# Hybrid decoder layer on one core: forms of the down projection and squared norms of the mixer, re-ordered

## The chip, the cores and the metric

One core of a Trainium2 chip runs the whole inference step as one program. The metric is device time in microseconds. The kernel is written with a scheduling layer: the program's functions emit instructions with priorities, the layer puts them into five in-order queues, one for each of TensorE (PE, matrix products), VectorE (DVE), ScalarE (ACT), GpSimd (POOL) and SyncE (SP, which issues nearly all DMAs), and adds the waits between them. An instruction that waits holds up all that stand behind it in its queue.

## The reference, cut to what matters

```
def l2_normalize(x):
    return x * lax.rsqrt(jnp.sum(x * x, axis=-1, keepdims=True) + 1e-6)
...
    q = l2_normalize(qkv[:, :, 0])                       # 4 heads x 128, after a short conv and silu
    k = l2_normalize(qkv[:, :, 1])
    o, s_new = gated_delta_chunked(q, k, v, g, beta, s0) # per head: triangular solve, then a scan over chunks
...
    x = x + jnp.square(jax.nn.relu(rms_norm(x, g_ff) @ w_up)) @ w_down
    x = x + (p @ w_ple) * jax.nn.sigmoid(rms_norm(x, g_ple) @ w_ple_gate)
```

There are 1024 prompt tokens and 8 sample tokens, the model width is 1024, the MLP is 4096 wide, all float32. The change touches three things in it: the norms of q and k in each of the four heads, the product with w_down, and the input embedding p.

## The kernel before, in words

Every float32 product is made as three reduced-precision products: a weight tile is split into a rounded part `whi` (a cast on ACT, L150) and a rest `wlo` (a subtraction on DVE, L153), the activations likewise, and PE adds hi·hi, lo·hi and hi·lo. A weight tile in this split pair is called a form (`form`, L169). The forms come out of a ring of four (`RING`), so ACT and DVE work a few tiles ahead of PE.

The mixing stage runs head by head inside the input projection. `weave` is a planner: it counts the PE time of the projection's matmuls and lets other generators ("tasks") emit their next piece when their due time, given by the costs that they yield (`NRM`, `RB_W`, `MRG` and others), has come. Hence the costs set the place of an instruction on every queue. For each head `gdn_gates` transposes k (and q) on PE, forms the sum of squares of every token in `ssf` (L564 adds the epsilon), takes a reciprocal root by 11 tiny DVE instructions (`rsqrt`, L248 to L254, called "the root" here), and multiplies by beta into `rkb`. PE transposes `rkb` (`rbT`, L578); from there a matrix `at` is built, `gdn_inverse` inverts its 32x32 blocks by 62 POOL instructions (L643, L644), writes the result to DRAM (`inv_d`), reads it back as `t`, transposes four blocks of it on DVE (L657, `STREAM_TRANSPOSE`) and merges the blocks by small matmuls (`m`, L667 and L676). `gdn_scan` then goes through eight chunks, with PE, DVE (`R` L716, `vn` L724, `st` L730) and ACT (`vk` L722) taking turns.

The down projection uses a fast scheme of seven half-size products for each quarter j of the 4096 rows: 28 products n = 0 to 27, in the order P1, P6, P7, P4, P2, P5, P3. Each product has four column blocks p, and each block is 24 matmuls. Its activations come from DRAM (`load_raw`, 1.06 MB in two halves), are cast on ACT (L1363) and their rest formed on DVE (L1364). Its weights are the raw quarter blocks A11, A21, A22, A12 (`load_a`, 1 MB each) or sums of them made on POOL: `s1` = A21+A22 (L1385) and `s2` = s1-A11 (L1386) for P6, `sd` (L1392) for P7 and P3. PE's and SP's order is the program's; ACT, DVE and POOL are ordered by the scheduler with `high_priority`, and by `tc.issue_after(x)`, which puts an instruction on its queue behind x.

While the products run, other work is woven in. The last two tiles of the up projection are still to be squared (`squared`, L1225, on ACT) and turned into differences (`dforms_of`, six POOL instructions, L1229 to L1231). The old residual comes in by `x1_old` (L1401, two DMAs of about 520 KB each, called for the four quarters C11, C21, C12, C22 of the result). After n = 12 the embedding p is loaded (`pt`, L1526), and each of its eight 128x256 pieces is scaled on POOL (L1530).

Of the kernel before, what the change touches and what calls it, by code (L numbers as in the profile page):

```python
# [9 lines left out]
F32 = mybir.dt.float32  # L10
# [7 lines left out]
P = 128  # L18
# [66 lines left out]
def trunk_step_kernel(  # L85
# [199 lines left out]
    with ExitStack() as mix:  # L285
# [255 lines left out]
        def gdn_gates(h, kq):  # L541

            q, k = kq[:, 1, :T], kq[:, 0, :T]
            hb = slice(h * NU, h * NU + NU)
            ck_put(h, 0, k)
            dt = sr.tile([P, T], F32, tag="dt", name="dt")
            SY.dma_start(dt, gc_d[h, :].partition_broadcast(P))
            ktok = sr.tile([P, T], F32, tag="kt", name="ktok")
            ssf = sm.tile([P, 2 * NU], F32, tag="ss", name="ssf")
            for j, src in ((0, k), (1, q)):  # L550
                for u0 in (0, 4):
                    ps = transposes(src, u0, "kT")
                    if j == 0:
                        V.tensor_copy(ktok[:, u0 * P : u0 * P + 512], ps)
                    for a in range(4):
                        u = u0 + a
                        sq = tn.tile([P, P], F32, tag="oq", bufs=1, name="sq")
                        x2 = ps[:, a * P : a * P + P] if j else ktok[:, u * P : u * P + P]
                        with tc.high_priority(PRI):
                            S.activation(sq, x2, AF.Square, accum_out=ssf[:, j * NU + u : j * NU + u + 1])  # L560
                    yield NRM
            ck_put(h, 2, ktok[:, :])
            with tc.high_priority(PRI):
                V.tensor_scalar_add(ssf, ssf, 1e-6)  # L564
                rkq = sm.tile([P, 2 * NU], F32, tag="rkq", bufs=4, name="rkq")
                rsqrt(sm, rkq, ssf, "rk")
                rk, rq = rkq[:, :NU], rkq[:, NU:]
                V.tensor_scalar_mul(rq, rq, P ** -0.5)
                rkb = sm.tile([P, NU], F32, tag="rkb", name="rkb")
                V.tensor_mul(rkb, rk, beta[:, h, :NU])  # L570
            nrke = sm.tile([P, NU], F32, tag="nrke", bufs=4, name="nrke")
            V.scalar_tensor_tensor(nrke, in0=rkb, scalar=-1.0, in1=eg[:, hb], op0=ALU.mult, op1=ALU.mult)
            rkl = sm.tile([P, NU], F32, tag="rkl", bufs=4, name="rkl")
            V.tensor_mul(rkl, rk, el[:, hb])
            gs[h] = dict(rq=rq, nrke=nrke, rkl=rkl)
            yield RB_W
            ps = pst("rbT", (NU, P))
            PE.transpose(ps, rkb, ident)  # L578
            rbr = sm.tile([NU, P], F32, tag="rbr", name="rbr")
            V.tensor_copy(rbr, ps)  # L580
            SY.dma_start(rb_d[h : h + 1, :].rearrange("o (u c) -> (o u) c", c=P), rbr)
            at = sr.tile([P, T], F32, tag="at", bufs=2, name="at")
            SY.dma_start(at, rb_d[h, :].partition_broadcast(P))
# [12 lines left out]
            for u in range(0, NU, 2):
                ps = pst("kk")
                for a in range(2):
                    c = slice((u + a) * P, (u + a + 1) * P)
                    PE.matmul(ps[:, a * 256 : a * 256 + 256], lhsT=k[:, c], rhs=kq[:, :, c], start=True, stop=True)  # L600
                for a in range(2):
                    c = slice((u + a) * P, (u + a + 1) * P)
                    r = rk[:, u + a : u + a + 1]
                    V.scalar_tensor_tensor(at[:, c], in0=ps[:, a * 256 : a * 256 + P], scalar=r, in1=at[:, c],
                                           op0=ALU.mult, op1=ALU.mult)
                    V.scalar_tensor_tensor(dt[:, c], in0=ps[:, a * 256 + P : a * 256 + 256], scalar=r, in1=dt[:, c],
                                           op0=ALU.mult, op1=ALU.mult)
# [16 lines left out]
        def gdn_inverse(h, at):  # L624
# [28 lines left out]
            td = [t64[Q[0], :, 0:32], t64[Q[1], :, 32:64], t64[Q[2], :, 0:32], t64[Q[3], :, 0:32]]  # L653
            for b in range(4):
                SY.dma_start(td[b], inv_d[1, h, b].rearrange("u i j -> i u j"))
            for b in range(4):
                V.transpose(sf3[Q[b], :, Q[b]], td[b])  # L657
            xp = sm.tile([P, NU, 64], F32, tag="xp", bufs=1, name="xp")

            def j32(ap):  # L660
# [716 lines left out]
    def down_forms():  # L1377
        for j in range(4):
            s1 = dst.tile([P, 4, 4, P], F32, tag="s1", name="s1")
            s2 = dst.tile([P, 4, 4, P], F32, tag="s2", name="s2")  # L1380
            for name, _ in DSTEPS:
                for p in range(4):
                    with tc.high_priority(PRI):
                        if name == "P6":
                            G.tensor_add(s1[:, p], a_of("A21", p), a_of("A22", p))  # L1385
                            placed["sum"] = G.tensor_sub(s2[:, p], s1[:, p], a_of("A11", p)).ins  # L1386
                            f = s2[:, p]
                        elif name == "P5":
                            f = s1[:, p]
                        elif name in ("P7", "P3"):  # L1390
                            f = dst.tile([P, 4, P], F32, tag="t", name="sd")
                            G.tensor_sub(f, *((a_of("A21", p), a_of("A11", p)) if name == "P7" else (a_of("A12", p), s2[:, p])))  # L1392
                        else:
                            f = a_of({"P1": "A11", "P4": "A22", "P2": "A12"}[name], p)
                        f = form(f)
# [53 lines left out]
        return q // 2 * 4 + 2 * nn + q % 2  # L1449

    def down():
        load_raw(0)
        load_a(0, "A11")
        load_a(0, "A21")
        load_a(0, "A22")
        x1_old(C11, 0, 0)
        split_raw(0)
        load_raw(1)
        source = down_forms()
# [1 line left out]
        for n, (j, i) in enumerate(seq):  # L1461
# [4 lines left out]
            for p in range(4):  # L1466
# [16 lines left out]
                f = next(source, None)  # L1483
                if f:
                    forms.append(f)
                if n == 1 and p < 2:
                    _, t, q = last[p]
                    with tc.issue_after(placed["cast", 1]):
                        squared(q)
                    with tc.issue_after(placed["sum"]):  # L1490
                        dforms_of(t, q, late[t])
                if j == 3:

# [23 lines left out]
                x1_old(C21, 1, 0)  # L1517
            elif n == 1:
                x1_old(C12, 0, 1)
            elif n == 2:  # L1520
                for p, t, q in last:
                    dforms_out(p, t, q, late[t])
            elif n == 3:
                x1_old(C22, 1, 1)
            elif n == 12:
                SY.dma_start(pt, p_prompt[0, 0].rearrange("(c p) d -> p c d", p=P))  # L1526
            elif 14 <= n < 18:
                for nn in range(2):
                    x = pt[:, pcol(nn, n - 14), :]
                    G.tensor_scalar_mul(x, x, mst[:, nn, n - 14 : n - 13])  # L1530
            if j < 3:
                for name in {1: ("A11", "A21"), 2: ("A22",), 5: ("A12",)}.get(i, ()):
                    load_a(j + 1, name)
# [275 lines left out]
```

## Time and profile before

| what | value |
|---|---|
| runs | 1405.53, 1400.80, 1403.98 us, median 1403.98 |
| profiled execution: time, span | 1404.94 us, 1403.2 us |
| busy | PE 94%, DVE 64%, POOL 51%, ACT 46% |
| mean granted TensorE clock | 0.971 |
| DMA | 194 MB, 138 GB/s on average |

PE is nearly always busy. What is left are some stalls of PE and stretches in which PE runs at the lower of its clock's two levels, 1.2 instead of 2.4 GHz (granted clock 0.50). In a row of a timeline the columns are the start, the duration, the engine, the line and the operation with its output and inputs; what stands in square brackets is how long the engine was idle just before, and what ended that.

### The profile page before, as it was taken

The numbers are of one execution on the slowest core, as the hardware profiler recorded it, in microseconds if no ns is written. First come the engines' busy times: TensorE is split into PE (matmuls) and PEld (weight loads), VectorE is DVE, ScalarE is ACT, GpSimd is POOL, SyncE is SP. The second block draws the span as 40 slices with busy tenths as digits, with TensorE's granted clock in tenths as the row PEclk, the third lists the DMA queues.
The fourth block names the chain that finished last, engine by engine and source line by source line (L and its number), as shares of the span: only waits on it lengthen the run. The fifth ranks groups of instructions, "written<-read, shape, count | busy, mean of one in ns | idle before, by whom it ended". The sixth has DMA issues, their size and how long they took to land.

```text
span 1403.2 us, 26599 instructions
## 1 busy us (share of the span) xinstructions
PE 1312.5 (94%) x10189; PEld 1280.5 (91%) x10189; DVE 900.7 (64%) x1836; ACT 645.6 (46%) x1353; POOL 708.8 (51%) x724
## 2 busy tenths in 40 slices
PE   6979978999999799899999999889998999899996
PEld 5879978888999799899999999889998999899996
DVE  7755745456946856555545544567976878797554
ACT  7574645632232415556545445443332333346344
POOL 5300888847515404668856787350516215835241
PEclk9999988999999999999999999999999999999998
DMA  7334534646524831244455564658353533232231
GB/s 237 101 91 107 153 92 137 177 135 174 150 84 146 259 90 46 61 137 130 150 149 169 175 212 155 221 191 283 117 184 113 172 122 121 61 102 78 63 121 61
DMA packets 213419, 194.00 MB, mean 138 GB/s; under 512 B 20952, under 2 KB 183451, under 8 KB 213284
## 3 DMA queue, kind: packets, MB, share of 16 engines
q1 hardware_dynamic: 213292, 192.30, 44.5%
q8 instruction: 80, 1.31, 0.4%
q14 instruction: 47, 0.39, 0.1%
HBM read 131.75 MB, written 60.61 MB: 137 GB/s over the span
## 4 chain that ended last, share of the span: by engine, by line
PE 69%; DVE 9%; POOL 9%; ACT 5%; issue 4%; DMA 3%; SPq 1%; POOLq 0%; ACTq 0%; DVEq 0%
PE A L1184 10%; PE D L1184 7%; PE d L1474 6%; PE d L1475 6%; PE d L1473 6%; PE g L209 5%; PE g L211 5%; PE g L210 5%; PE B L1184 3%; PE C L1184 3%; POOL xinv L644 2%; PE g L1702 2%; POOL it L643 2%; DVE wlo L153 2%; PE g L1704 2%
## 5 line engine op out<-in xcount | busy, mean ns | idle before, releaser
L209 PE MATMUL g<-ra,whi 128*128 128x384 f32 (+3 forms) x800 | 272.6, 341 | 0.7 <-ACT ra L388 0.6
L1474 PE MATMUL d<-h,wlo 128*128 128x260 f32 (+1 forms) x896 | 258.2, 288 | 11.0 <-DVE wlo L153 10.5
L1473 PE MATMUL d<-h,whi 128*128 128x260 f32 (+1 forms) x896 | 257.4, 287 | 7.9 <-ACT whi L150 7.9
L1475 PE MATMUL d<-h,whi 128*128 128x260 f32 (+1 forms) x896 | 257.3, 287 | 0.0
L211 PE MATMUL g<-ra,whi 128*128 128x384 f32 (+3 forms) x800 | 256.4, 321 | 0.8 <-POOL ra L389 0.4
L210 PE MATMUL g<-ra,wlo 128*128 128x384 f32 (+3 forms) x800 | 255.2, 319 | 0.0
L1474 PEld LDWEIGHTS d<-h,wlo 128*128 128x128 f32 x896 | 173.4, 194 | 13.3 <-DVE wlo L153 13.2
L1473 PEld LDWEIGHTS d<-h,whi 128*128 128x128 f32 x896 | 173.3, 193 | 8.9 <-ACT whi L150 8.9
L1475 PEld LDWEIGHTS d<-h,whi 128*128 128x128 f32 x896 | 173.2, 193 | 0.0
L209 PEld LDWEIGHTS g<-ra,whi 128*128 128x128 f32 x800 | 154.3, 193 | 2.9 <-ACT ra L388 1.0
L211 PEld LDWEIGHTS g<-ra,whi 128*128 128x128 f32 x800 | 153.7, 192 | 2.5 <-POOL ra L389 1.6
L210 PEld LDWEIGHTS g<-ra,wlo 128*128 128x128 f32 x800 | 154.7, 193 | 0.7 <-DVE wlo L153 0.3
L153 DVE TENSOR_TENSOR wlo<-s,whi 128x512 fp32r<-128x512 f32 x96 | 73.7, 769 | 80.8 <-ACT whi L150 80.4
L153 DVE TENSOR_TENSOR wlo<-st,whi 128x512 fp32r<-128x512 f32 x94 | 75.2, 801 | 39.9 <-ACT whi L150 39.1
L1184 PE MATMUL A<-fb,whi 128*128 128x260 f32 (+1 forms) x512 | 96.6, 281 | 0.0
L643 POOL TENSOR_TENSOR it<-ainv,xinv 32x31 f32<-32x31 f32 (+15 forms) x124 | 73.6, 594 | 39.6 <-DMA ainv<-inv_d 30.3
L150 ACT CAST whi<-s 128x512 fp32r<-128x512 f32 x96 | 59.3, 618 | 73.4 <-PE D L1184 29.1
L1363 ACT CAST h<-raw 128x1024 fp32r<-128x1024 f32 (+1 forms) x56 | 58.8, 1056 | 67.1 <-DMA raw<-f_d 34.7
L644 POOL TENSOR_TENSOR xinv<-xinv,it 32x31 f32<-32x31 f32 (+15 forms) x124 | 82.3, 664 | 9.6
L1225 ACT ACTIVATE q<-q 128x512 f32<-128x512 f32 (+2 forms) x124 | 77.5, 645 | 19.5 <-DVE q L1207 16.0
L1482 DVE TENSOR_TENSOR acc<-acc,d 128x256 f32<-128x256 f32 x192 | 75.0, 413 | 17.8 <-PE d L1475 16.8
L150 ACT CAST whi<-st 128x512 fp32r<-128x512 f32 x96 | 59.0, 619 | 58.2 <-PE g L211 31.4
(450 smaller groups left out, 3526.0 us busy)
## 6 DMA issues: line engine op xcount, KB each, us to landing
a<-in_w_down SPq DMA_DIRECT2D x16, 1024.0 KB
raw<-f_d SPq DMA_DIRECT2D x28, 520.0 KB
raw<-f_d SPq DMA_DIRECT2D x28, 512.0 KB
st<-in_w_in SPq DMA_DIRECT2D x24, 512.0 KB
ck<-ck_d SPq DMA_DIRECT2D x32, 320.0 KB
ra<-in_w_up SPq DMA_DIRECT2D x32, 256.0 KB
rb<-in_w_up SPq DMA_DIRECT2D x32, 256.0 KB
st<-in_w_ple_gate SPq DMA_DIRECT2D x16, 512.0 KB
```

The source lines that it names most:

```text
L150: S.copy(dst_hi, src)
L153: lo_eng.tensor_sub(dst_lo, src, f32(dst_hi))
L209: PE.matmul(ps[:, :w], lhsT=whi[k], rhs=xh, start=(k == 0), stop=False)
L210: PE.matmul(ps[:, :w], lhsT=wlo[k], rhs=xh, start=False, stop=False)
L211: PE.matmul(ps[:, :w], lhsT=whi[k], rhs=xl, start=False, stop=(k == nk - 1))
L643: G.tensor_mul(tv, a, x)
L644: G.tensor_sub(X[:, j + 1 :, :w], X[:, j + 1 :, :w], tv)
L1184: PE.matmul(ps, lhsT=a[:, k, :], rhs=x[:, c, k, :], start=(first and k == 0 and j == 0), stop=(k == 3 and j == 2), skip_group_check=True)
L1225: placed["act"] = S.activation(v, v, func).ins
L1473: PE.matmul(ps, lhsT=wh[:, k, :], rhs=xh[:, k, :], start=(k == 0), stop=False)
L1474: PE.matmul(ps, lhsT=wl[:, k, :], rhs=xh[:, k, :], start=False, stop=False)
L1475: PE.matmul(ps, lhsT=wh[:, k, :], rhs=xl[:, k, :], start=False, stop=(k == 3))
```

## The change

1. Mixing. The squared norms no longer come from 16 ACT squares with accumulation per head (over transposed 128x128 pieces). ACT squares k and q as a whole (128x1024 each, into `sq`, which takes the buffer that `qe` uses later), and PE multiplies each 128x128 piece of the squares with a column of ones: 16 matmuls of one column per head, into `ssq`. The eight transposes of q, which nothing else used, are gone. The task yields a new cost (`SQ` = 2.2) between the two.
2. Mixing. The four transposes of blocks on DVE in `gdn_inverse` are issued behind the last root that the program has emitted (`placed["root"]`, the multiplication into `rkb`).
3. Down projection, P6 of the first quarter: s1 and s2 are made in turn, block by block, where before the four s1 stood ahead of the four s2.
4. The squares and differences of the last two tiles of the up projection are made one product later, and stored after n = 3.
5. `x1_old(C11)` is issued ahead of the first loads of the down projection, where before it stood behind A22.
6. The embedding is scaled on ACT, two pieces for each of n = 14 to 17, behind the casts of that product.

```diff
-            for j, src in ((0, k), (1, q)):
-                for u0 in (0, 4):
-                    ps = transposes(src, u0, "kT")
...
-                            S.activation(sq, x2, AF.Square, accum_out=ssf[:, j * NU + u : j * NU + u + 1])
-                    yield NRM
+            sq = sr.tile([P, NT], F32, tag="kp", name="sq")
+            with tc.high_priority(PRI):
+                S.activation(sq[:, :T], k, AF.Square)
+            for u0 in (0, 4):
+                ps = transposes(k, u0, "kT")
+                V.tensor_copy(ktok[:, u0 * P : u0 * P + 512], ps)
+                yield NRM
...
+            tot = pst("ssq", (P, 2 * NU))
+            for j in range(2):
+                if j:
+                    with tc.high_priority(PRI):
+                        S.activation(sq[:, :T], q, AF.Square)
+                    yield SQ
+                for u in range(NU):
+                    PE.matmul(tot[:, j * NU + u : j * NU + u + 1], lhsT=sq[:, u * P : u * P + P], rhs=ones[:, 0:1], start=True, stop=True)
...
-            for b in range(4):
-                V.transpose(sf3[Q[b], :, Q[b]], td[b])
+            with tc.issue_after(placed["root"]):
+                for b in range(4):
+                    V.transpose(sf3[Q[b], :, Q[b]], td[b])
...
                         if name == "P6":
-                            G.tensor_add(s1[:, p], a_of("A21", p), a_of("A22", p))
+                            with tc.issue_after(placed["sum"]) if j == 0 and p else ExitStack():
+                                G.tensor_add(s1[:, p], a_of("A21", p), a_of("A22", p))
...
     def down():
+        x1_old(C11, 0, 0)
         load_raw(0)
         load_a(0, "A11")
         load_a(0, "A21")
         load_a(0, "A22")
-        x1_old(C11, 0, 0)
...
-                if n == 1 and p < 2:
+                if n == 2 and p < 2:
                     _, t, q = last[p]
-                    with tc.issue_after(placed["cast", 1]):
+                    with tc.issue_after(placed["cast", 2]):
                         squared(q)
-                    with tc.issue_after(placed["sum"]):
+                    with tc.issue_after(placed["sd"]):
                         dforms_of(t, q, late[t])
...
-                    G.tensor_scalar_mul(x, x, mst[:, nn, n - 14 : n - 13])
+                    with tc.issue_after(placed["cast", n]):
+                        S.activation(x, x, AF.Copy, scale=mst[:, nn, n - 14 : n - 13])
```

What the change does to three queues is shown by rows of their order; an `x4` at the end stands for four in a row.

POOL at the start of the down projection, before: `a_...` are the raw blocks, the first `s_...` is s1, the second s2, `acc<-q` are the differences of the last tiles.

```order
L1392 TENSOR_TENSOR sd<-a_11069,a_11072 128x512
L1385 TENSOR_TENSOR s_11090<-a_11069,a_11068 128x512 x4
L1386 TENSOR_TENSOR s_11091<-s_11090,a_11072 128x512 x4
L1229 TENSOR_TENSOR acc<-q_6118 128x2x256
L1230 TENSOR_TENSOR acc<-q_6118,acc 128x256
L1229 TENSOR_TENSOR acc<-q_6118 128x2x260
L1231 TENSOR_TENSOR acc<-q_6118,acc 128x256
L1230 TENSOR_TENSOR acc<-q_6118,acc 128x260
L1231 TENSOR_TENSOR acc<-q_6118,acc 128x260
L1392 TENSOR_TENSOR sd<-a_11069,a_11072 128x512 x3
L1392 TENSOR_TENSOR sd<-a_11067,s_11091 128x512
```

POOL there after the change:

```order
L1398 TENSOR_TENSOR sd<-a_10981,a_10984 128x512
L1391 TENSOR_TENSOR s_11002<-a_10981,a_10980 128x512
L1392 TENSOR_TENSOR s_11003<-s_11002,a_10984 128x512
L1391 TENSOR_TENSOR s_11002<-a_10981,a_10980 128x512
L1392 TENSOR_TENSOR s_11003<-s_11002,a_10984 128x512
L1391 TENSOR_TENSOR s_11002<-a_10981,a_10980 128x512
L1392 TENSOR_TENSOR s_11003<-s_11002,a_10984 128x512
L1391 TENSOR_TENSOR s_11002<-a_10981,a_10980 128x512
L1392 TENSOR_TENSOR s_11003<-s_11002,a_10984 128x512
L1398 TENSOR_TENSOR sd<-a_10981,a_10984 128x512 x3
L1234 TENSOR_TENSOR acc<-q_6030 128x2x256
L1234 TENSOR_TENSOR acc<-q_6030 128x2x260
```

The sums come in turn, the `sd` of P7 follow at once, and the six differences have moved behind them.

SP at the end of the up projection and the start of the down projection, before: `f_d<-q` and `f_d<-tt` store activations, `raw` and `a_...` are the loads of the first product, `acc<-x_d` is `x1_old(C11)`.

```order
L1237 DMA f_d<-tt 128x4x256
L1237 DMA f_d<-tt 128x4x260
L1356 DMA raw<-f_d 128x1024
L1356 DMA raw<-f_d 128x1040
L1372 DMA a_11072<-in_w_down 128x4x512
L1372 DMA a_11069<-in_w_down 128x4x512
L1372 DMA a_11068<-in_w_down 128x4x512
L1401 DMA acc<-x_d 128x4x256
L1401 DMA acc<-x_d 128x4x260
```

SP there after the change:

```order
L1242 DMA f_d<-tt 128x4x256
L1242 DMA f_d<-tt 128x4x260
L1407 DMA acc<-x_d 128x4x256
L1407 DMA acc<-x_d 128x4x260
L1361 DMA raw<-f_d 128x1024
L1361 DMA raw<-f_d 128x1040
L1377 DMA a_10984<-in_w_down 128x4x512
L1377 DMA a_10981<-in_w_down 128x4x512
L1377 DMA a_10980<-in_w_down 128x4x512
```

Nothing but `x1_old` has moved: five transfers past which it is issued.

DVE in the mixing stage, from the end of head 2's root on (its `rkt`, `rki`, `rkq`, `rkb`); the `STREAM_TRANSPOSE` rows are head 0's, `wlo` is a piece of the projection's weights, `dt<-dt,mneg` and `qe` belong to head 2. Before:

```order
L254 SCALAR_TENSOR_TENSOR rkq<-rkt,rki 128x16
L568 TENSOR_SCALAR rkq<-rkq 128x8
L570 TENSOR_TENSOR rkb<-rkq,beta 128x8
L589 TENSOR_TENSOR dt<-dt,mneg 128x1024
L574 TENSOR_TENSOR rkl<-rkq,el 128x8
L586 TENSOR_TENSOR qe<-qe,kq 128x1024
L572 SCALAR_TENSOR_TENSOR nrke<-rkb,eg 128x8
L748 TENSOR_TENSOR of<-rkq 128x8
L153 TENSOR_TENSOR wlo<-st,whi 128x512
L657 STREAM_TRANSPOSE sf<-t_2349 32x8x32
L153 TENSOR_TENSOR wlo<-st,whi 128x512
L657 STREAM_TRANSPOSE sf<-t_2349 32x8x32 x3
```

DVE there after the change:

```order
L594 TENSOR_TENSOR dt<-dt,mneg 128x1024
L591 TENSOR_TENSOR qe<-qe,kq 128x1024
L253 SCALAR_TENSOR_TENSOR rkt<-rki,ssf 128x16
L254 TENSOR_TENSOR rkt<-rkt,rki 128x16
L255 SCALAR_TENSOR_TENSOR rkq<-rkt,rki 128x16
L573 TENSOR_SCALAR rkq<-rkq 128x8
L575 TENSOR_TENSOR rkb<-rkq,beta 128x8
L579 TENSOR_TENSOR rkl<-rkq,el 128x8
L663 STREAM_TRANSPOSE sf<-t_2306 32x8x32 x2
L577 SCALAR_TENSOR_TENSOR nrke<-rkb,eg 128x8
L663 STREAM_TRANSPOSE sf<-t_2306 32x8x32
L754 TENSOR_TENSOR of<-rkq 128x8
```

`dt<-dt,mneg` and `qe` now stand inside the root, the first transposes follow right behind `rkb`, and the two `wlo` have moved behind the last of the four (the rows that come next), where one stood ahead of them all and one between them.

## Rows read from the trace of the kernel before

**Rows 1.** From the page: PE's busy time, and the share of each engine in the chain of work that ended last.

```profile
PE 1312.5 (94%) x10189; PEld 1280.5 (91%) x10189; DVE 900.7 (64%) x1836; ACT 645.6 (46%) x1353; POOL 708.8 (51%) x724
...
PE 69%; DVE 9%; POOL 9%; ACT 5%; issue 4%; DMA 3%; SPq 1%; POOLq 0%; ACTq 0%; DVEq 0%
```

**Rows 2.** PE's waits over the whole run: what waited, for what, total us, how often, the longest.

```profile
PE d L1474 <- DVE wlo L153: 10.5, 6, 4.8
...
PE d L1473 <- ACT whi L150: 7.9, 4, 4.7
PE rbT L578 <- DVE of L748: 7.7, 1, 7.7
...
PE m L667 <- DMA t<-inv_d: 5.0, 2, 3.8
```

**Rows 3.** Windows: start and end, length, then busy time and number of instructions of PE, PEld, DVE, ACT and POOL, the granted clock, the DMA share and GB/s. Six stretches behind stalls of PE, or behind many one- or two-column matmuls; the clock is the third number from the end.

```profile
104.60:109.70 5.10, 5.10 (x17) 5.10 (x18) 0.35 (x2) 0.00 (x0) 0.00 (x0) 0.50 0.33 103
...
337.50:345.00 7.50, 7.50 (x81) 7.34 (x81) 4.67 (x12) 2.01 (x5) 5.58 (x7) 1.00 0.60 168
...
703.60:707.10 3.50, 3.01 (x15) 2.50 (x15) 2.37 (x7) 1.10 (x3) 2.73 (x4) 0.51 0.66 186
910.00:915.20 5.20, 5.17 (x24) 5.18 (x25) 2.20 (x4) 0.00 (x0) 3.86 (x3) 0.50 1.07 388
928.90:932.30 3.40, 3.38 (x15) 3.38 (x16) 2.33 (x4) 1.06 (x1) 0.56 (x1) 0.50 0.98 344
1080.20:1085.90 5.70, 5.50 (x24) 5.21 (x25) 3.61 (x4) 1.66 (x3) 4.82 (x4) 0.50 0.43 130
```

**Rows 4.** Timeline of PE: the first matmul behind a stall in mixing and in the first two products, and the first and the last (24th) matmul of one column block of the down projection.

```profile
104.59 0.37 PE L578 MATMUL rbT<-ident,rkb 128*8 128x128 f32 x1 [7.67 <-DVE of L748]
...
199.46 1.03 PE L667 MATMUL m<-t,at 32*32 32x32 f32 x16 [3.81 <-DMA t<-inv_d]
...
910.02 0.58 PE L1474 MATMUL d<-h,wlo 128*128 128x256 f32 x1 [3.62 <-DVE wlo L153]
...
918.08 0.28 PE L1473 MATMUL d<-h,whi 128*128 128x256 f32 x1
...
920.84 0.28 PE L1475 MATMUL d<-h,whi 128*128 128x260 f32 x1
...
928.92 0.58 PE L1474 MATMUL d<-h,wlo 128*128 128x256 f32 x1 [4.80 <-DVE wlo L153]
```

**Rows 5.** Timeline of POOL at the start of the down projection.

```profile
911.34 5.29 POOL L1385 TENSOR_TENSOR s<-a,a 128x512 f32<-128x512 f32 x4 [1.92 <-DVE wlo L153]
916.59 5.07 POOL L1386 TENSOR_TENSOR s<-s,a 128x512 f32<-128x512 f32 x4
```

**Rows 6.** Timeline of ACT there.

```profile
895.69 0.37 ACT L1198 COPY u<-A 128x256 f32<-128x256 f32 x1 [0.73 <-PE A L1184]
...
905.35 2.18 ACT L150 CAST whi<-a 128x512 fp32r<-128x512 f32 x4 [1.66 <-DMA a<-in_w_down]
...
917.62 2.01 ACT L1225 ACTIVATE q<-q 128x1024 f32<-128x1024 f32 x2
919.54 1.12 ACT L150 CAST whi<-s 128x512 fp32r<-128x512 f32 x2
```

**Rows 7.** Timeline of DVE there.

```profile
908.22 3.56 DVE L153 TENSOR_TENSOR wlo<-a,whi 128x512 fp32r<-128x512 f32 x4
...
924.68 2.35 DVE L1364 TENSOR_TENSOR h<-raw,h 128x1040 fp32r<-128x1040 f32 x1
...
927.62 2.99 DVE L153 TENSOR_TENSOR wlo<-s,whi 128x512 fp32r<-128x512 f32 x3
```

**Rows 8.** The chain that ended last, in the stretch of n = 12 and n = 13: start, length, what.

```profile
1061.02 8.03 DMA q<-in_p_prompt
...
1069.14 9.18 POOL q L1530 x8
1078.32 1.24 POOL sd L1392
...
1079.58 0.62 ACT whi L150
...
1080.23 0.70 DVE wlo L153
```

**Rows 9.** Instructions that write or read tiles of these names: line, engine, operation, count, shortest/median/longest ns, first and last start.

```profile
L560 ACT ACTIVATE sq<-ktok x32: 293/311/315, 81.3 to 238.7; 128x128 f32<-128x128 f32 x32
...
L1274 PE MATMUL ms<-ones,ssu x20: 163/250/271, 701.3 to 703.3; 128*128 128x1 f32 x16, 128*4 128x1 f32 x4
...
L891 PE MATMUL sk<-kq_s,s x64: 165/251/251, 324.5 to 342.8; 128*128 128x2 f32 x64
```

**Rows 10.** Timeline of DVE in mixing: around head 0's root and head 3's root.

```profile
90.04 1.23 DVE L589 TENSOR_TENSOR dt<-dt,mneg 128x1024 f32<-128x1024 f32 x1 [5.62 <-ACT qe L585]
...
99.50 0.17 DVE L564 TENSOR_SCALAR ssf<-ssf 128x16 f32<-128x16 f32 x1
...
235.47 0.25 DVE L853 COPY xx<-tail 128x96 f32<-128x96 f32 x1 [3.15 <-POOL tail L518]
...
247.06 0.29 DVE L724 COPY vn<-cb 128x128 f32<-128x128 f32 x1 [1.19 <-ACT vk L722]
...
249.43 1.40 DVE L589 TENSOR_TENSOR dt<-dt,mneg 128x1024 f32<-128x1024 f32 x1 [0.35 <-ACT qe L585]
```

More of the change, by code (lines that the diff above doesn't have):

```diff
@@ L64 @@
 NRM = 0.6
+SQ = 2.2
 KKS = 0.8
@@ L534, in trunk_step_kernel @@
         gs = {}
+        placed = {}
         gated = []
@@ L549, in gdn_gates @@
             ssf = sm.tile([P, 2 * NU], F32, tag="ss", name="ssf")
-            for j, src in ((0, k), (1, q)):
-                for u0 in (0, 4):
-                    ps = transposes(src, u0, "kT")
[L553 to L559, printed above, removed]
-                            S.activation(sq, x2, AF.Square, accum_out=ssf[:, j * NU + u : j * NU + u + 1])
-                    yield NRM
-            ck_put(h, 2, ktok[:, :])
+            sq = sr.tile([P, NT], F32, tag="kp", name="sq")
[5 more added lines that the diff above has]
+                yield NRM
+            ck_put(h, 2, ktok[:, :])
+            tot = pst("ssq", (P, 2 * NU))
[6 more added lines that the diff above has]
+                    PE.matmul(tot[:, j * NU + u : j * NU + u + 1], lhsT=sq[:, u * P : u * P + P], rhs=ones[:, 0:1], start=True, stop=True)
             with tc.high_priority(PRI):
-                V.tensor_scalar_add(ssf, ssf, 1e-6)
+                V.tensor_scalar_add(ssf, tot, 1e-6)
                 rkq = sm.tile([P, 2 * NU], F32, tag="rkq", bufs=4, name="rkq")
@@ L569, in gdn_gates @@
                 rkb = sm.tile([P, NU], F32, tag="rkb", name="rkb")
-                V.tensor_mul(rkb, rk, beta[:, h, :NU])
+                placed["root"] = V.tensor_mul(rkb, rk, beta[:, h, :NU]).ins
             nrke = sm.tile([P, NU], F32, tag="nrke", bufs=4, name="nrke")
@@ L1217, in up_stage @@
                 yield 3 * w * 0.000455
-    placed = {}
     last = []
@@ L1391, in down_forms @@
                             f = dst.tile([P, 4, P], F32, tag="t", name="sd")
-                            G.tensor_sub(f, *((a_of("A21", p), a_of("A11", p)) if name == "P7" else (a_of("A12", p), s2[:, p])))
+                            placed["sd"] = G.tensor_sub(f, *((a_of("A21", p), a_of("A11", p)) if name == "P7" else (a_of("A12", p), s2[:, p]))).ins
                         else:
@@ L1519, in down @@
                 x1_old(C12, 0, 1)
-            elif n == 2:
+            elif n == 3:
                 for p, t, q in last:
                     dforms_out(p, t, q, late[t])
-            elif n == 3:
                 x1_old(C22, 1, 1)
```

## The prediction

> **What bounds the kernel now.** I read the page first: PE is busy 94% of the span and makes up 69% of the chain that ended last, and no other engine comes near [rows 1]. So the time is the sum of PE's stream, PE's stalls, and what PE loses at the lower clock. The waits of PE come next [rows 2]: most lost time is in a few single waits, and the change touches the places of three of them, the 4.8 us for a `wlo`, the 4.7 us for a `whi`, the 7.7 us at `rbT`. Third, the windows [rows 3]: behind each of these stalls the granted clock is 0.50 for 3.4 to 5.7 us, and work there takes twice as long, so half of such a stretch is lost on top. At the full clock the 24 matmuls of a column block start within 918.08 to 920.84, 0.12 us apart [rows 4], so a block takes 2.88 us and a product 11.5.
>
> **P6 of the first quarter (n = 1).** PE waits 4.80 us for a `wlo<-s` [rows 4] and loses 3.4/2 = 1.7 at the low clock [rows 3]: 6.5. The cause can be followed back. POOL makes four s1 in 5.29 and four s2 in 5.07 us [rows 5], so the first s2 comes 5.29 + 1.27 = 6.6 us after A22 is there. ACT has squares of 2.01 us (two) between the casts `whi<-s` [rows 6]. DVE makes a `h` of 2.35 us, and only at 927.62 the `wlo<-s` [rows 7]. In turn, a pair of s1 and s2 takes 2.6 us, less than a block's 2.88: the first s2 is ready 4.0 us sooner after A22, 1.3 sooner if A22 lands 2.7 later (below), and the following keep up with PE. The squares then stand behind three of the four casts. I estimate the first two pairs of `whi` and `wlo` done some 2 us ahead of PE and the last two 1 to 2 us ahead, since they stand behind the next product's casts and `h`, which wait for a transfer. I take 0.9 us as left, so 5.6 gained; bounds 3 (two of the four late by a stall of 1.2 us and its slow stretch) and 6.5. The six differences behind the P7 `sd` cost nothing: POOL then has no form to make before the third P7 block. Without that cover a block would wait one difference, 1 to 1.5 us.
>
> **The embedding on ACT (n = 13).** The chain shows it whole: the transfer lands at 1069.05, eight scalings hold POOL for 9.18 us, then `sd` 1.24, `whi` 0.62, `wlo` 0.70 and PE [rows 8]. PE stalls 4.7 [rows 2] and loses 5.7/2 = 2.85 [rows 3]: 7.5. Without the scalings `sd` goes on at 1068.7. But one link of `sd`, `whi`, `wlo` takes 1.24 + 0.62 + 0.70 plus handovers, about 2.7 against PE's 2.88, which leaves little room; I keep 1.3 as lost and gain 6.2 (bounds 4 and 7.5). On ACT a copy of this size takes 0.37 [rows 6], two per product, and ACT stands idle more than half of the time; were it not, 0.75 us per product would stand ahead of a `whi`, four times.
>
> **x1_old first.** Its 1.06 MB take 2.7 us at the 388 GB/s of the full queue [rows 3]. All of raw, A11, A21 and A22 then land up to 2.7 us later. The first `whi<-a` moves from 905.35 [rows 6] to 908.1. Yet PE's second matmul waited until 910.02 [rows 4], because DVE reached `wlo<-a` at 908.22 only [rows 7] and took 0.9 for each beside a POOL `sd`. With `whi` at 908.7 the `wlo` comes at 909.4 to 910.4, as before. Cost 0 to 0.3; bounds -0.5 and +2.7 (the whole delay). In the Trainium skill, the page DMA: Bandwidth & Descriptors (Queues, rings and completion order) says that each DMA engine consumes SP's descriptors in ring order. By it x1_old goes ahead of all five loads and the 2.7 us are paid in full at A11; the trace agrees as far as it shows loads landing in the order of issue, and the rival below prices the case.
>
> **Mixing.** Per head 16 squares of 0.3 us each [rows 9] with their reads leave ACT, two of about 1.0, as for the same size in [rows 6], come. PE loses eight transposes and gets 16 one-column matmuls, 0.105 us apart by the 20 `ms` (701.3 to 703.3) [rows 9]; with the transposes at the same pace that is 0.8 us more per head, 3.4 in all. Those 20 were followed by a clock of 0.51, while 64 two-column `sk` were not [rows 3, 9]; groups of eight I take as harmless (bound: four times 1.7).
>
> Head 0's root could not begin before 99.50, since ACT's last square came that late [rows 10], and PE stood 7.67 us at `rbT` [rows 4] and lost 5.1/2 = 2.55 [rows 3]. With ACT relieved I estimate `rkb` at about 94, some 4 us ahead of PE. That gives 7.67 + 2.55 - 0.8 = 9.4 at this place.
>
> Most of it is given back, since what follows hangs on other chains. (a) POOL's inverse and its two transfers shift with the stream, so PE's wait of 3.81 at `m` [rows 4] stays. (b) The transposes, pinned behind head 2's root, wait for `t`, and two `wlo` and the conv steps of kq are queued behind them on DVE, then `xp` on ACT: some 3 us. (c) `xx<-tail` already holds DVE 3.15 us for POOL's tail copy [rows 10], which stands about five POOL instructions later in the new order: 1 us. (d) In head 3 `dt<-dt,mneg` and `qe` (1.4 and 1.2 us) now stand in the middle of the root, ahead of the scan's `vn`, which came at 247.06 while `dt` was not free before 249.43 [rows 10]: 2 to 3 us. The other three heads' matmuls take 2.4 more, part of it under PE's waits. Of 9.4 I keep 2.5; bounds 9 gained (nothing of b to d on PE's path) and 5 lost.
>
> **Sum.** -5.6 - 6.2 + 0.2 - 2.5 = -14.1, against the profiled execution's 1404.94: 1390.8. The runs' median of 1403.98 is 1.0 lower; I say 1390.
>
> **Rivals.**
> 1. The gain of head 0 stays (8.5 of 9.4): the steps b to d fall into time in which PE has projection work anyway. For it: in [rows 10] it is DVE that waits, and for long. Against it: the wait at `m` shows that PE can run out of such work. 1404.9 - 11.6 - 8.5 = 1384.8.
> 2. The start of the down projection pays: x1_old ahead costs 2.7 at n = 0, and the late A22 leaves half of n = 1's stall. For it: the queue is full there (DMA share 1.07 [rows 3]). Against it: DVE was the later one. -2.8 - 6.2 + 2.7 - 2.5 = -8.8: 1396.
> 3. The edit at n = 13 doesn't do what it says: the links of 2.7 us are all that PE gets, and a smaller stall stays. -5.6 - 3 + 0.2 - 2.5 = -10.9: 1394.
> 4. Slower: `dt<-dt,mneg` inside the root. It waits for ACT's `qe`; in head 0 DVE stood 5.62 us there [rows 10]. Inside the root such a wait delays `rkb`, and with it `rbT` on PE. If each of heads 1 to 3 pays these 5.6 and half of a slow stretch of 5.1, 8.15 us, 24.5 come, and of head 0's 9.4 some 5 go as well: -11.6 + 24.5 - 4.4 = +8.5, that is 1413. From 6.7 us per head on the kernel is slower by over 0.3%. Against it: ACT, rid of the squares, should make `qe` sooner than before.
>
> **How the numbers follow.** About 0.3% (4.2 us) is what a measurement of this kernel can tell from no change. Chances: forecast (1386 to 1394) 0.52, first rival 0.18, second 0.13, third 0.08, fourth 0.05 and cases between it and the second 0.04. The range reaches from the first rival with nothing left of the stalls at n = 1 and n = 13 (1382.6) to 1399, the second rival with a little more lost in mixing. Faster: all but the fourth and those between, 0.89, less 0.02 for a poor second: 0.87. The rest is shared: 0.08 same, 0.05 slower.
>
> **What the profile would show.** Right: no PE stall over 2 us at n = 1 and n = 13, a granted clock of 1.00 there; `rbT` no longer among PE's long waits; the wait at `m` still 2 to 4 us; at n = 0 PE waiting for `whi<-a` and matmuls running from about 910. Wrong would be: a stall at `rbT` of heads 1 to 3; `wlo<-s` still behind `h` on DVE when PE wants it; clock 0.50 behind the groups of eight; a late x1_old(C22), now issued behind n = 3, which holds DVE's additions and so PE.

## The result, and the profile after

The changed kernel takes 1395.7 us (median of 11 runs, 1391.4 to 1401.0) against 1405.1 for the kernel before on the same chips (11 runs): a ratio of 0.9937, 95% interval 0.9922 to 0.9951, 9 us faster. The forecast was 1390, range 1381 to 1399. The profiled execution of the changed kernel took 1399.9 us, 4 above its median, its span 1398.2.

The page's busy times come first, those of PE against [rows 1]:

```profile
PE 1321.6 (95%) x10285; PEld 1292.2 (92%) x10285; DVE 901.6 (64%) x1836; ACT 630.4 (45%) x1238; POOL 702.3 (50%) x716
```

PE has 96 instructions and 9.1 us of busy time more than before; busy time counts the stretches at the lower clock at their full length. Its waits over the whole run, which answer to [rows 2]:

```profile
PE cb L741 <- DVE vn L730: 11.2, 5, 4.3
PE d L1479 <- ACT whi L151: 6.7, 4, 3.5
...
PE cb L742 <- DVE vn L730: 4.7, 1, 4.7
PE d L1480 <- DVE wlo L154: 4.1, 5, 2.1
...
PE g L211 <- DVE wlo L154: 3.3, 1, 3.3
PE m L682 <- ACT xp L676: 2.6, 1, 2.6
PE cb L725 <- DVE R L722: 2.5, 3, 1.3
```

The waits of the scans (`cb`) in the kernel before, for comparison:

```profile
PE cb L719 <- DVE R L716: 9.3, 5, 3.0
...
PE cb L736 <- DVE vn L724: 4.2, 1, 4.2
...
PE cb L735 <- DVE vn L724: 3.4, 5, 1.1
```

The 7.7 us at `rbT` are gone, and the products' waits for `whi` and `wlo` have shrunk from 7.9 and 10.5 to 6.7 and 4.1 us (`d` at L1479, L1480). The waits for `t` at `m` [rows 2] are gone too, and a new one of 3.3 us for a `wlo` of the input projection has come. The scans wait longer for `vn` (15.9 us instead of 7.6) and less for `R` (2.5 instead of 9.3): in sum 18.4 us, where it was 16.9.

The windows of the first products, of n = 6 (two) and of n = 13, read as those of [rows 3]:

```profile
914.50:921.30 6.80, 6.33 (x28) 6.04 (x28) 3.64 (x8) 2.64 (x5) 3.46 (x3) 0.50 0.93 364
921.40:940.00 18.60, 18.60 (x158) 18.60 (x157) 16.38 (x29) 10.58 (x14) 13.18 (x8) 1.00 0.68 233
994.00:996.30 2.30, 0.23 (x2) 0.02 (x1) 2.30 (x5) 0.00 (x0) 0.00 (x0) 1.00 0.00 0
996.40:999.80 3.40, 3.40 (x16) 3.40 (x17) 2.35 (x5) 1.66 (x3) 3.32 (x3) 0.50 0.24 42
1072.40:1084.40 12.00, 11.81 (x98) 11.43 (x97) 9.99 (x15) 4.84 (x9) 8.21 (x6) 1.00 0.30 102
```

The clock is still 0.50 at n = 0 and is 1.00 through n = 1, where PE is now busy all the time. At n = 13 it is 1.00 too, and PE stands for 0.19 us. At n = 6 there is a stall that was not there in this size before, and the low clock behind it.

Times of the products, from the first matmul of one to the first of the next (n = 0 counted from the last matmul of the up projection, so with the stall ahead of it), in the one profiled execution of each kernel; the medians and ratios are of all runs:

| kernel | median us | ratio to before, interval | n = 0 | n = 1 | n = 6 | n = 13 |
|---|---|---|---|---|---|---|
| before | 1405.1 | | 18.6 | 18.0 | 13.3 | 19.2 |
| changed | 1395.7 | 0.9937, 0.9922 to 0.9951 | 18.6 | 11.4 | 16.7 | 12.1 |
| e1 down only | 1396.8 | 0.9930, 0.9905 to 0.9956 | 16.9 | 11.4 | 18.0 | 12.1 |
| e2 mixing only | 1407.6 | 1.0011, 0.9996 to 1.0027 | 18.8 | 17.6 | 12.1 | 18.4 |
| e3 products for head 0 | 1388.6 | 0.9882, 0.9857 to 0.9907 | 19.2 | 11.4 | 15.9 | 12.1 |
| e4 rounded norms, 8 B | 1396.1 | 0.9939, 0.9916 to 0.9962 | 18.0 | 11.4 | 15.9 | 12.1 |
| e5 rounded norms, 64 B | 1397.1 | 0.9953, 0.9936 to 0.9970 | 18.9 | 11.5 | 15.4 | 12.1 |
| e6 8 B unused | 1400.0 | 0.9967, 0.9951 to 0.9983 | 16.5 | 11.4 | 17.9 | 12.1 |
| e7 not in turn | 1396.0 | 0.9940, 0.9921 to 0.9959 | 18.0 | 13.8 | 14.4 | 12.1 |
| e8 not late | 1396.3 | 0.9935, 0.9913 to 0.9958 | 16.8 | 12.8 | 12.9 | 12.1 |
| e9 x1_old back | 1397.9 | 0.9941, 0.9920 to 0.9963 | 18.7 | 11.9 | 16.4 | 12.1 |
| e10 unpinned | 1395.8 | 0.9926, 0.9903 to 0.9950 | 16.7 | 11.4 | 17.9 | 12.1 |
| e11 head 0, all in turn | 1381.5 | 0.9827, 0.9802 to 0.9852 | 19.3 | 11.4 | 12.1 | 11.4 |

The kernel before came out between 1404.8 and 1406.3 in the sessions, so kernels of different sessions are compared by their ratios. One run of e9, 1828.4 us at a granted clock of 0.652, is left out of its median and ratio.

### The profile page after: what moved, and what is told of

The parts are those of the page before. It is cut to its first block, busy times and chain, and to the rows that moved or that the text cites. A ratio compares the mean times of both kernels' runs of the same rounds, so it can differ in the third digit from the quotient of the medians.

```text
span 1398.2 us, 26676 instructions
## 1 busy us (share of the span) xinstructions
PE 1321.6 (95%) x10285; PEld 1292.2 (92%) x10285; DVE 901.6 (64%) x1836; ACT 630.4 (45%) x1238; POOL 702.3 (50%) x716
## 4 chain that ended last, share of the span: by engine, by line
PE 67%; POOL 11%; DVE 10%; issue 5%; DMA 4%; ACT 2%; SPq 1%; POOLq 0%; DVEq 0%; ACTq 0%
PE A L1190 9%; PE D L1190 6%; PE d L1480 6%; PE d L1481 6%; PE d L1479 6%; PE g L210 5%; PE g L212 5%; PE g L211 5%; POOL it L648 3%; POOL xinv L649 3%; PE C L1190 3%; PE B L1190 3%; DVE wlo L154 2%; PE g L1708 2%; PE g L1710 2%
## 5 line engine op out<-in xcount | busy, mean ns | idle before, releaser
L1479 PE MATMUL d<-h,whi 128*128 128x260 f32 (+1 forms) x896 | 256.4, 286 | 6.7 <-ACT whi L151 6.7
L1480 PE MATMUL d<-h,wlo 128*128 128x260 f32 (+1 forms) x896 | 257.1, 287 | 4.6 <-DVE wlo L154 4.1
L1479 PEld LDWEIGHTS d<-h,whi 128*128 128x128 f32 x896 | 172.4, 192 | 7.6 <-ACT whi L151 7.6
L1480 PEld LDWEIGHTS d<-h,wlo 128*128 128x128 f32 x896 | 172.4, 192 | 6.6 <-DVE wlo L154 6.5
L1488 DVE TENSOR_TENSOR acc<-acc,d 128x256 f32<-128x256 f32 x192 | 75.2, 413 | 17.3 <-PE d L1481 16.4
```

What stands on the lines that cost most here:

```text
L1479: PE.matmul(ps, lhsT=wh[:, k, :], rhs=xh[:, k, :], start=(k == 0), stop=False)
L1480: PE.matmul(ps, lhsT=wl[:, k, :], rhs=xh[:, k, :], start=False, stop=False)
```

## The experiments

**The two halves apart.** e1 keeps the changed down projection and puts the old mixing back; e2 the other way round.

> Only the four edits of the down projection; mixing as before. If the down projection's share is what the trace of the changed kernel shows (n = 1 6.5 and n = 13 7.0 us shorter, n = 6 3.5 longer), the time is 10.3 us below before, 1394 to 1396, and hence all of the change's gain. If mixing had a gain of its own (2.5 as forecast), this kernel would be some 2.5 us slower than the changed one.

> Only the mixing edits; down projection as before. Theory A (PE pays for the squared norms): 10.2 us gained at head 0's rbT against 10.8 us of added products on PE, 0 to +2 us against before, 1404 to 1407. By the forecast: -2.5, 1402.5. PE busy about 9 us above before in both.

e1 is 9.8 us faster than before (ratio 0.9930), the whole gain of the change. e2 is 1.5 us slower, with an interval from 0.6 faster to 3.8 slower. So mixing brings no gain that could be seen. Yet the stall at head 0's `rbT` is gone; in the changed kernel `rkb` is ready well ahead, and PE's `rbT` (the second fence) starts with no idle time before it, where it stood 7.67 us [rows 4]:

```profile
89.49 0.17 DVE L569 TENSOR_SCALAR ssf<-ssq 128x16 f32<-128x16 f32 x1 [3.96 <-PE ssq L567]
...
95.73 0.16 DVE L575 TENSOR_TENSOR rkb<-rkq,beta 128x8 f32<-128x8 f32 x1
```

```profile
101.04 0.27 PE L583 MATMUL rbT<-ident,rkb 128*8 128x128 f32 x1
```

What took it back shows in PE's own stream. The first head's transposes and squared norms on PE:

```profile
80.22 0.60 PE L529 MATMUL kT<-ident,kq 128*128 128x128 f32 x4
80.57 0.42 PE L210 MATMUL g<-ra,whi 128*128 128x384 f32 x1
...
83.21 1.84 PE L567 MATMUL ssq<-ones,sq 128*128 128x1 f32 x16
84.91 0.42 PE L210 MATMUL g<-ra,whi 128*128 128x384 f32 x1
```

The trace counts 16 matmuls where the program has eight: these float32 products are carried out as two instructions each, 0.106 us per instruction in the mean, though a product has one column. A group of eight takes 84.91 - 83.21 = 1.70 us, a head 3.4; four transposes take 80.57 - 80.22 = 0.35, so the eight removed ones 0.70. PE pays 2.7 us per head, 10.8 in all, against 10.2 for head 0's stall and slow stretch.

**The price of the squared norms.** If this is the reason, then heads 1 to 3, which had no stall of more than 1.5 us at `rbT`, should get their ACT squares back:

```diff
-            sq = sr.tile(...)                      # squares whole, transposes of k, 16 products
-            ...
+            if h == 0:
+                sq = sr.tile(...)                  # as in the changed kernel
+                ...
+            else:
+                tot = ssf
+                for j, src in ((0, k), (1, q)):    # as before
+                ...
```

> The changed kernel, with the squared norms as products for head 0 only; heads 1 to 3 square on ACT and transpose q on PE as before. Theory A: PE is rid of 3 x 2.7 = 8.1 us, and the time falls by 4 to 8 us below the changed kernel's, to 1388 to 1392. Theory B (the gain of head 0 went into new waits on DVE, the products lie under them): no change, 1394 to 1397, with the waits at vn of heads 1 to 3 as long as before or longer.

The ratio falls to 0.9882, about 7.7 us below that of the changed kernel, and the two intervals do not meet. A part of the 7.7 goes with the clock: the runs' median granted clock is 0.978 here, 0.975 in the changed kernel. But among runs of both at 0.977 to 0.980 this version takes 1387.2 to 1389.4 us, the changed kernel 1391.4 to 1394.5. In the profiles PE is busy 15.6 us less. The products of three heads are 8.1 of them; how much of the rest is less work at the low clock (the mean granted clock is 0.978 against 0.970 in these two executions) was not separated. ACT takes 15 us more without harm:

```profile
PE 1306.0 (94%) x10213; PEld 1276.2 (92%) x10213; DVE 900.1 (65%) x1836; ACT 645.5 (47%) x1331; POOL 704.8 (51%) x716
```

So theory A holds, and theory B (new waits ate the gain) falls: against e1 (0.9930) this version shows what mixing is worth with one head's products, 6.7 us of the 7.5 that 10.2 - 2.7 would give; the two intervals overlap a little, so the 6.7 are rough.

The same price was tried in another way, by a rounded format in which a product is one instruction:

```diff
+    onesr = cst.tile([P, 2], F32R, name="onesr")
+    V.tensor_copy(onesr, ones[:, 0:2])
...
-                    PE.matmul(tot[:, j * NU + u : j * NU + u + 1], lhsT=sq[:, u * P : u * P + P], rhs=ones[:, 0:1], start=True, stop=True)
+                    PE.matmul(tot[:, 2 * (j * NU + u) : 2 * (j * NU + u) + 2], lhsT=sq[:, u * P : u * P + P], rhs=onesr, start=True, stop=True)
```

> The changed kernel, with the squares and the ones in the rounded format and two columns of ones in place of one (the compiler refuses one), so that a product is one instruction instead of two: the squared norms are then of rounded squares. Theory A: PE has 64 instructions of 0.106 us less, 6.8 us, and the time falls by 4 to 7 us, to 1389 to 1392. Theory B: no change, 1394 to 1397.

The 64 instructions were gone, but the time did not move (1396.1), as theory B had it. In the profile e4 entered the up projection 6.6 us ahead of the changed kernel and left it 2 us ahead, at the same order of matmuls. How much of the 6.6 the norms gave is open, since the changed kernel's profile entered late (583.6 us, where e2, e7, e8 and e9 with the same mixing entered at 579.5 to 582.4). The loss within the up projection stands out: about a microsecond of it lies in a stretch at a clock of 0.50 (705.9 to 709.3 us), the rest at 1.00. The difference left there was where tiles lie: the new tile of 8 bytes per partition shifts all that are laid out behind it. e5 holds the same column in 64 bytes, e6 has nothing but an unused tile of 8 bytes.

> The squared norms as in the run with rounded squares, but the column of ones is held in a tile of 64 bytes per partition instead of 8, so that the tiles laid out behind it keep their places modulo 64 bytes. In the run with 8 bytes PE's up projection ran 1.35% slower all along (from 6.6 us ahead of the changed kernel at 616 us to 2.0 ahead at 896) at the same order and clock. If the place of the tiles does that, this run keeps the 6.6 us: 1388 to 1391, and the up projection takes as long as in the changed kernel. If it was that chip or execution, the slope is there in some runs only; if rounded squares save nothing, 1394 to 1397.

> The changed kernel with nothing but an unused tile of 8 bytes per partition ahead of the other tiles. If the place of the tiles sets PE's pace, the up projection takes some 4 to 5 us longer than in the changed kernel and the down projection's products 11.30 us each instead of 11.28 and 11.41 in turn: 1398 to 1401. If not, 1394 to 1397.

e6 shows that the unused tile alone slows PE; the whole kernel takes 4 us longer (0.9967 against 0.9937, the intervals meet at 0.9951). A window of the changed kernel, and the same of e6 (second fence), in the up projection:

```profile
750.00:800.00 50.00, 50.00 (x426) 50.00 (x425) 24.42 (x41) 25.38 (x49) 39.86 (x33) 1.00 0.57 180
```

```profile
750.00:800.00 50.00, 50.00 (x420) 50.00 (x419) 22.48 (x38) 23.74 (x46) 42.10 (x35) 1.00 0.61 194
```

PE is busy all the time at full clock in both, and does 426 matmuls in 50 us in the one, 420 in the other. From its 301st matmul to its last the up projection takes 285.0 us in the nine profiles of kernels laid out as the changed one, 288.3 in e5, 288.6 in e6 and 289.8 in e4 (with its stretch at 0.50). My guess of 64 bytes as the step that matters was wrong: e5 runs at the slow pace too, and at 0.9953 is no faster than the changed kernel. Held against e6, which has the same 8 bytes, e4 is 0.28% or 3.9 us faster, with intervals that overlap a little: in the direction of theory A, at the low end of its 4 to 7, and not shown by itself. Which places of which tiles set the pace stays open.

**What each edit at n = 1 does, and n = 6.** In the changed kernel DVE and ACT show why n = 6 stalls. DVE, then ACT:

```profile
990.36 0.69 DVE L154 TENSOR_TENSOR wlo<-sd,whi 128x512 fp32r<-128x512 f32 x1 [1.01 <-ACT whi L151]
991.31 2.21 DVE L1369 TENSOR_TENSOR h<-raw,h 128x1024 fp32r<-128x1024 f32 x1 [0.26 <-ACT h L1368]
...
994.11 1.23 DVE L1369 TENSOR_TENSOR h<-raw,h 128x1040 fp32r<-128x1040 f32 x1
...
995.59 0.68 DVE L154 TENSOR_TENSOR wlo<-sd,whi 128x512 fp32r<-128x512 f32 x1
```

```profile
989.71 0.62 ACT L151 CAST whi<-sd 128x512 fp32r<-128x512 f32 x1 [7.72 <-POOL sd L1398]
990.23 2.01 ACT L1368 CAST h<-raw 128x1024 fp32r<-128x1024 f32 x2
992.47 0.62 ACT L151 CAST whi<-sd 128x512 fp32r<-128x512 f32 x1 [0.22 <-POOL sd L1398]
```

The third `whi<-sd` is made at 992.47, but its `wlo` comes only at 995.59, behind two `h` of the next product, which had their casts (2.01 us) ahead of that `whi` on ACT. In the kernel before, the casts of `h` stood one ahead of and one behind the second `whi` (988.71):

```profile
986.33 1.05 ACT L1363 CAST h<-raw 128x1024 fp32r<-128x1024 f32 x1 [5.98 <-PE d L1474]
988.71 0.62 ACT L150 CAST whi<-sd 128x512 fp32r<-128x512 f32 x1 [1.33 <-POOL sd L1392]
989.23 1.05 ACT L1363 CAST h<-raw 128x1040 fp32r<-128x1040 f32 x1
```

Nobody edited this place: the scheduler chose the order, and came to another choice once the work before it had moved. e7 takes the sums in turn away, e8 the lateness:

```diff
-                            with tc.issue_after(placed["sum"]) if j == 0 and p else ExitStack():     # e7
-                                G.tensor_add(s1[:, p], a_of("A21", p), a_of("A22", p))
+                            G.tensor_add(s1[:, p], a_of("A21", p), a_of("A22", p))
...
-                if n == 2 and p < 2:                                                                  # e8
+                if n == 1 and p < 2:
```

> The changed kernel with the four s1 ahead of the four s2 again. Theory: the stall at n = 6 comes from the order that the sums in turn leave behind them on ACT (two casts of h ahead of the second whi of P3), so n = 6 takes 12 to 13 us again instead of 16; and at n = 1 the late squares alone leave half of the gain: n = 1 takes 13 to 16 us instead of 11.3. In all -3.5 + 2 to 5: 1394 to 1398. Rival: the sums in turn do nothing at n = 1, the late squares all: n = 1 stays at 11.3, and the time falls to 1391 to 1393.

> The changed kernel with the last squares and differences made at n = 1 again, the sums still in turn. Theory: squares between the whi casts and the differences on POOL make n = 1 lose 2 to 5 us again, n = 6 stays at 16: 1397 to 1401. Rival: the sums in turn alone give all of n = 1's gain: 1394 to 1397, n = 1 at 11.3.

Of the 6.6 us that n = 1 gains with both edits (11.4), either edit alone gives a part: n = 1 takes 13.8 with the squares late, 12.8 with the sums in turn, but then n = 2 takes 13.6 instead of 11.5. What the second edit adds there, 2.4 to 3.5 us, is paid at n = 6, which is 14.4 and 12.9 with one edit and 16.7 with both. The three times are the same within their intervals. e7 went as its theory had it, with n = 6 only partly back. e8 did not: n = 1 lost 1.4 us and n = 2 2.1 us, in sum what the theory had for n = 1, but n = 6 fell too, and the time (1396.3) is the rival's, though not its n = 1 of 11.3.

e8 also shows that the order on ACT is not the whole cause. Two casts of `h` stand ahead of the third `whi` there as well, yet n = 6 takes 12.9. POOL tells the two apart. The changed kernel, where n = 6 starts at 986.8, then e8 (at 985.9; POOL and ACT), then the kernel before (at 987.7):

```profile
981.93 6.49 POOL L1391 TENSOR_TENSOR s<-a,a 128x512 f32<-128x512 f32 x4 [26.14 <-DVE wlo L154]
988.38 1.30 POOL L1398 TENSOR_TENSOR sd<-a,s 128x512 f32<-128x512 f32 x1
```

```profile
984.71 1.30 POOL L1398 TENSOR_TENSOR sd<-a,s 128x512 f32<-128x512 f32 x1
...
986.57 2.01 ACT L1368 CAST h<-raw 128x1024 fp32r<-128x1024 f32 x2
```

```profile
987.37 1.31 POOL L1392 TENSOR_TENSOR sd<-a,s 128x512 f32<-128x512 f32 x1
```

In the changed kernel POOL comes to the second `sd` of P3 1.5 us after n = 6 has started, since the four s1 of the next quarter stand ahead of it; in e8 it comes 1.2 us before, in the kernel before 0.3 us before. All 13 profiles go the same way: n = 6 takes 12.1 to 13.3 where that `sd` starts before n = 6 does, and 14.4 to 18.0 where it starts 0.4 to 2.8 us after. In e7 ACT has the old order again, and the `sd` starts 0.4 us after. So the late `sd` and the order on ACT both play a part; e11 below moves the s1 away. What sets the time at which POOL starts these s1 was not followed.

**The place of x1_old.**

> The changed kernel with x1_old(C11) behind A22 again. By the forecast its place costs nothing (0 to 0.3): PE's first down products end no sooner, 1394 to 1397; the first whi<-a comes 2.7 us sooner and DVE is then the later one. By the second rival it costs 2.7: 1392 to 1393, with n = 0 and the stall ahead of it together 2.7 us shorter.

n = 0 with its stall takes 18.7 with x1_old at the old place, 18.6 at the new, and the time is the same (0.9941). ACT's first `whi<-a`, with x1_old back, then in the changed kernel:

```profile
907.17 2.18 ACT L151 CAST whi<-a 128x512 fp32r<-128x512 f32 x4 [1.66 <-DMA a<-in_w_down]
```

```profile
914.15 2.18 ACT L151 CAST whi<-a 128x512 fp32r<-128x512 f32 x4 [1.69 <-DMA a<-in_w_down]
```

The up projection's last matmul begins at 906.9 in the one and 911.0 in the other, so `whi<-a` comes 0.25 us after it in the one and 3.1 in the other: x1_old does hold the loads back by 2.9 us. What hides it is DVE, the later one of the two before. PE's first matmuls, with x1_old back, then in the changed kernel:

```profile
907.84 0.38 PE L1479 MATMUL d<-h,whi 128*128 128x256 f32 x1 [0.64 <-ACT whi L151]
...
911.68 0.58 PE L1480 MATMUL d<-h,wlo 128*128 128x256 f32 x1 [3.45 <-DVE wlo L154]
```

```profile
914.83 0.58 PE L1479 MATMUL d<-h,whi 128*128 128x256 f32 x1 [3.52 <-ACT whi L151]
```

With x1_old back, PE starts early and then stands 3.45 us for the first `wlo`; in the changed kernel it stands 3.52 us for the `whi`, and no longer for a `wlo`. Among kernels with the same down projection n = 0 varies from 16.5 to 19.2, and the times' intervals are 0.2% wide on either side, so a cost of a microsecond could not be seen.

**The pins.**

> The changed kernel with the four transposes on DVE free of the root. By the forecast (step b of what mixing gives back) the pins hold back two wlo and the conv steps and cost up to 3 us: 1392 to 1394, and PE's wait for a wlo in the projection (3.3 us near 197) is gone. Rival: the pins only order what waits for t anyway: 1394 to 1397.

The time is the rival's (1395.8), but neither had the mechanism. The wait for the `wlo` is gone, and another has come:

```profile
PE rbT L583 <- DVE rkl L579: 9.9, 1, 9.9
```

```profile
184.86 0.41 DVE L253 SCALAR_TENSOR_TENSOR rkt<-rki,ssf 128x16 f32<-128x16 f32 x1
193.55 0.43 DVE L662 STREAM_TRANSPOSE sf<-t 32x256 f32<-32x256 f32 x1 [8.27 <-DMA t<-inv_d]
...
195.67 0.15 DVE L575 TENSOR_TENSOR rkb<-rkq,beta 128x8 f32<-128x8 f32 x1
```

Free of the pin, the first transpose of head 0 is queued in the middle of head 2's root, stands there 8.27 us until `t` has landed, and holds up `rkb` (195.67) and with it `rbT` on PE for 9.9 us. With the pin the transposes wait behind `rkb` and hold up the `wlo` instead. Without it PE's waits of 3.3 us for the `wlo` and of 2.6 us for `xp` at `m` are gone, and the 9.9 us at `rbT` have come. The time is the same within the intervals (0.9926), so the pin moves the waits; a gain or loss of 2 or 3 us could not be seen.

**A version that beats both.** e11 is e3 with the sums of all quarters in turn, those of a later quarter behind the last `sd` of the quarter before.

```diff
-                            with tc.issue_after(placed["sum"]) if j == 0 and p else ExitStack():
+                            with tc.issue_after(placed["sum"] if p else placed["sd"]) if j or p else ExitStack():
```

> The version with products for head 0 only, and the sums of the later quarters in turn as well and behind the last sd of the quarter before. If the s1 that POOL makes ahead of P3's sd, and the order on ACT that follows, make the stall at n = 6, n = 6 falls from 15.9 to 12 or 13 us: 1384 to 1386. If the stall comes from the casts of h alone, no change: 1387 to 1390.

n = 6 falls to 12.1, and the products of the same kind at n = 13 and n = 20 to 11.4 and 11.5 (from 12.1 each). POOL and PE's waits show it:

```profile
976.28 1.30 POOL L1414 TENSOR_TENSOR sd<-a,s 128x512 f32<-128x512 f32 x1 [28.86 <-DVE wlo L154]
979.05 1.30 POOL L1414 TENSOR_TENSOR sd<-a,s 128x512 f32<-128x512 f32 x1 [1.46 <-DVE wlo L154]
982.79 2.24 POOL L1414 TENSOR_TENSOR sd<-a,s 128x512 f32<-128x512 f32 x1 [2.44 <-DVE wlo L154]
984.98 1.29 POOL L1407 TENSOR_TENSOR s<-a,a 128x512 f32<-128x512 f32 x1
```

```profile
PE d L1496 <- DVE wlo L154: 1.8, 3, 0.8
```

The `sd` follow one another with no s1 ahead of them (the first one shown starts 1.3 us before n = 6), and 1.8 us in all are left of the products' waits for a `wlo`. So the s1 ahead of P3's `sd`, with the order on ACT that follows from them, made the stall. The time, 1381.5, is 2.5 us below the forecast range; the products from n = 1 to n = 26 account for 5.7 of the 7.7 us that e11 is below e3. The ratio is 0.9827 (0.9802 to 0.9852), 24 us below the kernel before.

## Why the prediction was right, and where not

The time lay in the range, and the forecast of a clear gain held, but of the 14.1 us only 9 came. That the time is as near as this is in part luck: two terms of mixing were wrong in opposite directions. Against the forecast, the products cost 7.4 us more and n = 6 3.5 more, while n = 1 and n = 13 gave 1.9 more, and the 4.5 us that steps a to d were to take back (9.4 - 2.4 - 2.5 in the prediction's terms) were not seen. That makes -14.1 + 7.4 + 3.5 - 1.9 - 4.5 = -9.6. Step by step:

- **n = 1: right, a little small.** 5.6 forecast, 18.0 - 11.4 = 6.6 measured. The two edits share it, and each alone leaves 2.4 to 3.5 us of it at n = 1 and n = 2.
- **n = 13: right.** 6.2 forecast, 19.2 - 12.1 = 7.1 measured; the third rival, that the link of `sd`, `whi` and `wlo` leaves a stall there, did not come true at n = 13.
- **n = 6: not foreseen.** A stall in the same chain of `sd`, `whi` and `wlo` came at the P3 of the first quarter instead, 3.5 us beyond before in the profiles of the two kernels, but not from the links alone: POOL came late to the `sd`, and two `h` stood ahead of a `wlo`. The prediction followed the queues only where the diff has its edits. The down projection as a whole gave 10 where 11.6 were forecast.
- **x1_old: right**, by the cover named: loads 2.9 us later (2.7 forecast), no cost that could be seen. The ring order that the Trainium skill's page DMA: Bandwidth & Descriptors (Queues, rings and completion order) states agrees with these 2.9 us, but its price didn't reach PE; the second rival falls.
- **Mixing: the term that was mis-sized.** The 16 one-column matmuls per head, put at "0.8 us more per head, 3.4 in all", cost 2.7 per head and 10.8 in all. I took the count of instructions in the row of `ms` for the count of products [rows 9]; the trace shows 20 for the program's ten `ms`, and 64 for 32 `sk`, so a float32 product is two instructions here, and the row had shown it. This alone is 7.4 us, more than the 5 that are missing.
- **What mixing gives back: wrong, in the other direction.** Most of head 0's gain was to be lost in steps a to d. e3 keeps some 6.7 of 7.5. The wait for `t` at `m`, which was to stay (a), is not in the trace of the changed kernel; one of 2.6 us for `xp` is. The wait at the `wlo` (b) did appear, 3.3 us, and the scans do wait longer for `vn` (d), but less for `R`, and e10 shows that taking the pin away only moved the waits. The first rival's mechanism fits best here, at another price of the products: -10.2 + 10.8 = +0.6, beside the 1.5 that e2 measured (0.6 faster to 3.8 slower).
- **The fourth rival**, the slower side, didn't come: `rbT` of heads 1 to 3 doesn't appear among PE's waits of the changed kernel. e10 shows the mechanism at full size all the same, with the transposes in the root in place of `dt`.
- **A slip in the chances.** Those of all cases but the fourth rival and the ones between it and the second add up to 0.91, not 0.89.

## What to carry to other kernels

Count what the engine executes, not what the program calls: a price per instruction has to be multiplied by the instructions that a row shows for one call, and a reduction moved onto the engine that bounds the kernel pays only where a stall of that engine stands behind it, here in one head of four. Where a scheduler sets the order, an edit at one place can move queues thousands of instructions later, so the order has to be read at every place with as little room as the edited one. An interleaving that helps in the first round may be wanted in all rounds. And a total near the forecast says little about its terms: here two that were wrong by 7.4 and 4.5 us partly cancelled.

## What the runs showed of the hardware

I had not expected that an unused tile of 8 bytes per partition slows PE: the up projection then does 420 matmuls in 50 us instead of 426, busy throughout and at a granted clock of 1.00, and the whole kernel takes 4 us longer (e6); with 64 bytes the pace is the slow one too (e5). So kernels whose tiles lie at other places should not be compared to within 0.3%. Groups of eight one-column products (16 instructions in 1.70 us) left the clock at 1.00 in head 0, as taken in the forecast:

```profile
80.00:84.00 4.00, 4.00 (x31) 3.88 (x30) 3.93 (x7) 0.50 (x3) 0.00 (x0) 1.00 0.48 135
84.00:88.00 4.00, 4.00 (x30) 4.00 (x29) 1.39 (x3) 2.88 (x4) 0.00 (x0) 1.00 0.68 170
88.00:92.00 4.00, 4.00 (x31) 4.00 (x31) 0.96 (x6) 3.34 (x4) 0.00 (x0) 1.00 0.32 96
```
